# Layer 2: the queries' low parts on 128 rows through DMA copies, multiplies on GpSimd, another order of work; layer 3: the minimum that starts from the sink

## The chip, the cores and the metric

The kernel runs on one core of one Trainium2 chip. The metric is the device time of one execution in microseconds. In the texts TensorE (PE in the profile; its weight loads are PEld) multiplies matrices, VectorE (DVE), ScalarE (ACT) and GpSimd (POOL) work on vectors, and SyncE (SP) issues most of the DMAs. Each of them works through its own queue in order.

## What is computed

The kernel computes two blocks behind each other, of two layers each, on 512 tokens of width 1024 (32-bit floats): layer 1 (a gated recurrence and pooling), layer 2 (attention over the best keys), then layer 3 (attention in a window, with sinks), a feed-forward layer, layer 4 (three kinds of attention) and a second feed-forward layer. The change touches layers 2 and 3. Of the reference, layer 2 in its core:

```python
q = rmsnorm(q.reshape(hd), g_q)                 # 16 heads of 64
ckv = rmsnorm(ckv, g_kv)                        # rank 256
k = rmsnorm((ckv @ w_uk).reshape(hd), g_k)
v = (ckv @ w_uv).reshape(hd)
...
score = jnp.where((key_pos[None, :] <= t[:, None])[None], score, -jnp.inf)
_, idx = lax.top_k(score, top_k)                # 128 keys for each query
...
logits = jnp.einsum('bqhd,bqkhd->bqhk', qb, ksel).astype(jnp.float32) * (C_HEAD_DIM ** -0.5)
logits = logits + bias.transpose(0, 1, 3, 2)
logits = jnp.where(valid[:, :, None, :], logits, -jnp.inf)
probs = jax.nn.softmax(logits, axis=-1).astype(v.dtype)
return jnp.einsum('bqhk,bqkhd->bqhd', probs, vsel)
...
return x + (out * jax.nn.silu(z)) @ w_out
```

and layer 3 in its core (a window of 128 keys; `sk` is the sink, one number for each head):

```python
m = jnp.maximum(jnp.max(s, axis=-1, keepdims=True), sk)
e = jnp.exp(s - m)
p = e / (jnp.sum(e, axis=-1, keepdims=True) + jnp.exp(sk - m))
return jnp.einsum('bhgqs,bshd->bqhgd', p.astype(vn.dtype), vn)
```

## The kernel before

Matmuls are made of two halves of each number. An operand is split into a high part (h) and a low part (l), and a dense product is three matmuls: high by high, low by high, high by low (lines 148 to 150). Weights come by DMA from SP into `raw` (line 124), ScalarE writes the high part `wh` (line 129) and another engine subtracts for the low part `wl` (line 130); in layers 2 and 3 that engine is GpSimd. There are two `raw` buffers and four pairs of `wh` and `wl`.

Layer 2 is `odd`. TensorE's order is the order in which the code is written; the other engines' order follows from a scheduler. A `Filler` holds a list of work items (projections of queries, keys, values and gates, and parts of the output product), and `f.fill(n)` lets TensorE do the next n parts of it. An item's weights are asked for when the item before it begins. `mid` hangs a function between two parts of an item, here the transposes `q_t` and `k_t`, which bring queries and keys to feature-major form (`to_feature`, line 960: TensorE transposes, line 965, then the split). Between the parts stands first the choice of the keys (`topk`: 16 rounds of a maximum and a replacement on VectorE, lines 895 and 896), which ends in a mask for each block of 128 queries, and then the attention.

Queries and keys leave the projection token-major. `head_scale` (line 933) squares them (ScalarE), adds up (VectorE), takes the power -0.5 on GpSimd (`rr`, line 293) and multiplies by it (line 955).

The attention goes by units: one unit is one head and one half of the queries (256 rows: two blocks of 128), 32 units in all, by four groups g of four heads. Half 0 has 128 and 256 keys for its two blocks, half 1 has 384 and 512. The first group takes its eight units half by half, the later ones pair by pair. In step s of the loop TensorE does the logits of unit s, then two parts of the filler, the values of unit s - 3, the transposes of the probabilities of unit s - 2, and two parts again. `attend` (line 714) has the logits, the reduction with the bias strip (line 736), the exponential (line 738), the reciprocal (line 740) and the scaling by it, of the first block on VectorE (line 742) and of the second on ScalarE (line 743).

A head has 64 rows. The keys tile of one head `kT[g][j][r]` holds its high part in 64 rows and its low part in the other 64. A logit tile is two matmuls (`qk2r`, line 776): the high part of the queries, doubled over 128 rows (`qd`), by the whole keys tile, and the low part, 64 rows, by the high part of the keys:

```python
pe.matmul(lg, qd[:, o:o + P], k[:, :S], start=True, stop=False)
pe.matmul(lg, ql[rows, bs], k[rows, :S], start=False, stop=stop)
```

`query_twice` (line 1128) makes `qd` by two GpSimd copies of 64 x 256 a unit (line 1135), one unit ahead, into two buffers. Where queries are masked, a bf16 matmul adds the mask (line 732).

Layer 3 is `swa`; its units (`unit`, line 1287) are one head and one half, 32 again. GpSimd puts the negated sink `nsk` into a column beside the logits (line 1295), VectorE reduces each block with the strip to its minimum (all is negated; line 1304), takes the minimum with the sink (line 1306), ScalarE makes the exponentials (line 1309), VectorE the reciprocal (line 1310) and the scaling of both blocks (line 1313); TensorE transposes them three units later (line 1318).

Of the kernel before, what the change touches and what calls it, by code (L numbers as in the profile page):

```python
# [11 lines left out]
F32R = mybir.dt.float32r  # L12
# [4 lines left out]
P = 128  # L17
# [9 lines left out]
def f32(ap):  # L27
    return ap.bitcast(F32)
# [3 lines left out]
def kernel(ctx: ExitStack, tc: tile.TileContext, a: dict, out: bass.AP, upto: int = 9, start: int = 1):  # L32
# [681 lines left out]
    def attend(half, lp, qk, strip, probs, mask=None, gate=None, lbufs=2):  # L714
# [24 lines left out]
            Ls.append(L)  # L739
        dve.reciprocal(sm[:, 4:6], sm[:, 2:4])  # L740
        if gate is None:
            dve.tensor_scalar(Ls[0], Ls[0], sm[:, 4:5], None, op0=ALU.mult)
            act.activation(Ls[1], Ls[1], AF.Copy, scale=sm[:, 5:6])
        else:
            for ii in range(2):
                (dve if ii == half else pool).tensor_scalar(Ls[ii], Ls[ii], sm[:, 4 + ii:5 + ii], gate(i0 + ii),
                                                            op0=ALU.mult, op1=ALU.mult)
# [25 lines left out]
                pe.matmul(dst[:, :, 256 - w:], vv(b), p[:, :, 256 * b:256 * b + w], start=start and x + b == 0,  # L773
                          stop=stop and x == 1 and b == nb - 1)

    def qk2r(qd, ql, k, r, half):


        rows = slice(64 * r, 64 * r + 64)

        def f(lg, i, S, stop):
            bs, o = slice(i * P, (i + 1) * P), (i - 2 * half) * P
            pe.matmul(lg, qd[:, o:o + P], k[:, :S], start=True, stop=False)
            pe.matmul(lg, ql[rows, bs], k[rows, :S], start=False, stop=stop)
        return f

    def qk2(q, k):
# [21 lines left out]


    def odd(n):
        es, lp, tmp = open_layer("l2", 0, 0, 5, dict(mm=2, at=2, lg=2, po=2), weng=[pool])
        use_mm("lg", "po")

        def rt(name):
# [117 lines left out]
        def head_scale(ps, name, pre):  # L933
# [18 lines left out]
                dve.tensor_mul(r4, r4, pre[:, 0:NB, None].to_broadcast([P, NB, 4]))  # L952
            for x in range(2):
                t8 = tt[x].rearrange("p (h d) -> p h d", d=64)
                dve.tensor_mul(t8, t8, r[:, 8 * x:8 * x + 8, None].to_broadcast([P, 8, 64]))
            return [t[:, o:o + 256] for t in tt for o in (0, 256)]

        kT, qT, vv = {}, {}, {}
# [106 lines left out]
        with tc.manual_schedule(engines={pe.engine}):  # L1065
# [10 lines left out]
            def k_t(g, j):  # L1076
                return to_feature("kt", kT, g, gqk, j)

            f = Filler([proj(3, index_query), proj(0, latent), proj(1, latent), queries(0), keys(0), zgate(0),
                        mid(zgate(1), {2: q_t(0, 0), 5: q_t(0, 1)}), mid(zgate(2), {1: k_t(0, 0), 5: k_t(0, 1)}),  # L1080
                        values(0), zgate(3), zgate(4), zgate(5),
                        keys(1), mid(queries(1), {11: k_t(1, 0), 15: k_t(1, 1)}), values(1), keys(2),
                        mid(queries(2), {0: q_t(1, 0), 12: q_t(1, 1), 13: k_t(2, 0), 15: k_t(2, 1)}), values(2),
                        mid(out_part(0, 0), {4: q_t(2, 0)}), mid(out_part(0, 1), {2: q_t(2, 1)}), keys(3),
                        mid(queries(3), {10: k_t(3, 0), 11: k_t(3, 1)}), values(3),
                        mid(out_part(1, 0), {2: q_t(3, 0), 4: q_t(3, 1)}), zgate(6), out_part(1, 1), zgate(7),
                        out_part(2, 0), out_part(2, 1)])
            n.rtm
            f.fill(7)
# [38 lines left out]
            def query_twice(s):  # L1128
                if s in qd or s >= len(units) or len(qT.get(units[s][0], ())) <= units[s][1]:
                    return  # L1130
                g, j, half, r = units[s]
                rows = slice(64 * r, 64 * r + 64)
                t = qd[s] = lp.tile([P, 256], F32R, tag="qd", name="qd", bufs=2)
                for x in range(2):
                    pool.tensor_copy(t[64 * x:64 * x + 64], qT[g][j][0][rows, 256 * half:256 * half + 256])

            for s in range(len(units) + 3):
                query_twice(s)
                if s < len(units):
                    g, j, half, r = units[s]  # L1140
                    w = 256 * (half + 1)
                    stp = lp.tile([P, w], F32, tag=f"stp{half}", name="stp", bufs=2)
                    nc.sync.dma_start(stp, strip_ap(0, 4 * g + 2 * j + r, 1, T - w, w))

                    def probs(s=s, half=half):
                        pr[s] = prob_tiles(lp, half, 1, 1)
                        return [p[:, 0] for p in pr[s]]

                    live.append(attend(half, lp, qk2r(qd.pop(s), qT[g][j][1], kT[g][j][r], r, half), stp, probs,
                                       masks, lbufs=2))  # L1150
                    next(live[s])
                f.fill(2 if s < 24 else 1.4)
                query_twice(s + 1)
                if s >= 3:
                    u = s - 3
                    g, j, half, r = units[u]
# [64 lines left out]
    def swa(n):  # L1221
# [65 lines left out]
        def unit(j, r, half):  # L1287
# [13 lines left out]
                pe.matmul(d, q[r][:, bs], k[0][:, ks], start=True, stop=False)  # L1301
                pe.matmul(d, q[r][:, bs], k[1][:, ks], start=False, stop=True)
            for ii, (c0, S) in enumerate(where):
                dve.tensor_tensor_reduce(LL[:, c0 + ii:c0 + ii + S], lg[:, c0:c0 + S], strip[:, h, 256 - S:], 1.0, -NEG,
                                         op0=ALU.add, op1=ALU.min, accum_out=sm[:, ii:ii + 1])
            dve.tensor_scalar(sm[:, 0:2], sm[:, 0:2], nsk[:, h:h + 1], None, op0=ALU.min)
            for ii, (c0, S) in enumerate(where):
                L = LL[:, c0 + ii:c0 + ii + S + 1]
                act.activation(L, L, AF.Exp, scale=-1.0, bias=sm[:, ii:ii + 1], accum_out=sm[:, 2 + ii:3 + ii])
            dve.reciprocal(sm[:, 6:8], sm[:, 2:4])  # L1310
            for ii, (c0, S) in enumerate(where):
                L = LL[:, c0 + ii:c0 + ii + S]
                dve.tensor_scalar(L, L, sm[:, 6 + ii:7 + ii], None, op0=ALU.mult)
            yield
            pt = ps_at("pt")
            for x in range(3 + half):
# [711 lines left out]
```

## Time and profile before

| | us |
|---|---|
| three runs | 1972.92, 1973.52, 1975.42 (median 1973.52) |
| the profiled execution | 1972.96 |
| its span, first to last instruction | 1970.9 |
| busy: TensorE | 1917.8 (97%) |
| busy: VectorE | 1292.7 (66%) |
| busy: ScalarE | 964.6 (49%) |
| busy: GpSimd | 532.8 (27%) |

A busy share is a mean over stages with different limits, so it has to be asked for stage by stage. Layer 2 lies between about 490 and 780 us of the span, its attention between 570 and 760; layer 3's attention lies between 820 and 920. [...] Matmuls lie over each other, so what one costs is read from its start to the start of the next. A wait is put down to the instruction that came last.

### The profile page before, as it was taken

The numbers are of one execution on the slowest core, as the hardware profiler recorded it, in microseconds if no ns is written. First come the engines' busy times: TensorE is split into PE (matmuls) and PEld (weight loads), VectorE is DVE, ScalarE is ACT, GpSimd is POOL, SyncE is SP. The second block draws the span as 40 slices with busy tenths as digits, with TensorE's granted clock in tenths as the row PEclk, the third lists the DMA queues.
The fourth block names the chain that finished last, engine by engine and source line by source line (L and its number), as shares of the span: only waits on it lengthen the run. The fifth ranks groups of instructions, "written<-read, shape, count | busy, mean of one in ns | idle before, by whom it ended". The sixth has DMA issues, their size and how long they took to land.

```text
span 1970.9 us, 27008 instructions
## 1 busy us (share of the span) xinstructions
PE 1917.8 (97%) x9669; PEld 1595.5 (81%) x9678; DVE 1292.7 (66%) x2679; ACT 964.6 (49%) x1976; POOL 532.8 (27%) x612
## 2 busy tenths in 40 slices
PE   9999999999899999899999999998999999999998
PEld 7888888887787877777888888887888888888887
DVE  6776667556997777597654454456999765445443
ACT  5543343434447776586432232345888653323233
POOL 1101011025554545654200000044666440000002
PEclk9999999999999999899999999999999999999999
DMA  4233332213233332211423223233211132322321
GB/s 160 90 109 106 126 112 97 97 65 102 83 106 94 98 94 99 92 53 33 140 96 96 93 93 98 76 126 104 71 44 39 43 134 93 96 95 96 97 80 59
DMA packets 62063, 181.37 MB, mean 92 GB/s; under 512 B 7077, under 2 KB 13477, under 8 KB 61929
## 3 DMA queue, kind: packets, MB, share of 16 engines
q1 hardware_dynamic: 58200, 175.90, 28.0%
q10 hardware_dynamic: 3728, 3.75, 0.6%
q8 instruction: 76, 1.25, 0.3%
q14 instruction: 59, 0.48, 0.1%
HBM read 167.03 MB, written 12.59 MB: 91 GB/s over the span
## 4 chain that ended last, share of the span: by engine, by line
PE 83%; DVE 12%; ACT 2%; issue 1%; POOL 1%; DMA 1%; DVEq 0%; ACTq 0%; POOLq 0%
PE pj L148 6%; PE pj L149 6%; PE pj L150 6%; PE pg L149 4%; PE pg L148 4%; PE pg L150 4%; PE pu L149 4%; PE pu L148 4%; PE pu L150 4%; PE dn L149 4%; PE dn L148 4%; PE dn L150 4%; PE wo L148 3%; PE wo L150 3%; PE wo L149 3%; PE po L773 2%
## 5 line engine op out<-in xcount | busy, mean ns | idle before, releaser
L129 ACT CAST wh<-raw 128x512 fp32r<-128x512 f32 (+1 forms) x582 | 354.2, 613 | 620.4 <-PE pu L149 140.5
L130 DVE TENSOR_TENSOR wl<-raw,wh 128x512 fp32r<-128x512 f32 (+2 forms) x425 | 291.2, 689 | 189.8 <-ACT wh L129 187.6
L148 PE MATMUL pj<-xh,wh 128*128 128x512 f32 (+1 forms) x648 | 267.2, 413 | 2.1 <-DVE gx L1570 1.6
L150 PE MATMUL pj<-xh,wl 128*128 128x512 f32 (+1 forms) x648 | 257.1, 397 | 2.9 <-POOL wl L130 2.9
L149 PE MATMUL pj<-xl,wh 128*128 128x512 f32 (+1 forms) x648 | 257.2, 397 | 1.5 <-DVE xl L277 1.5
L130 POOL TENSOR_TENSOR wl<-raw,wh 128x512 fp32r<-128x512 f32 x157 | 208.0, 1328 | 172.9 <-ACT wh L129 156.9
L150 PEld LDWEIGHTS pj<-xh,wl 128*128 128x128 f32 (+1 forms) x648 | 122.8, 190 | 31.9 <-POOL wl L130 3.7
L285 POOL TENSOR_TENSOR sq<-sq 128x512 f32<-128x512 f32 x30 | 47.5, 1582 | 366.7 <-ACT sq L283 366.3
L148 PEld LDWEIGHTS pj<-xh,wh 128*128 128x128 f32 (+1 forms) x648 | 123.6, 191 | 24.8 <-ACT wh L129 2.0
L149 PEld LDWEIGHTS pj<-xl,wh 128*128 128x128 f32 (+1 forms) x648 | 123.4, 190 | 24.8 <-DVE xl L277 2.9
L149 PE MATMUL dn<-hl,wh 128*128 128x512 f32 (+1 forms) x376 | 141.6, 377 | 0.0
L148 PE MATMUL dn<-hh,wh 128*128 128x512 f32 (+1 forms) x376 | 141.2, 377 | 0.0
L150 PE MATMUL dn<-hh,wl 128*128 128x512 f32 (+1 forms) x376 | 140.7, 375 | 0.0
L148 PE MATMUL pg<-xh,wh 128*128 128x512 f32 x352 | 138.2, 393 | 0.0
L149 PE MATMUL pg<-xl,wh 128*128 128x512 f32 x352 | 138.2, 393 | 0.0
L150 PE MATMUL pg<-xh,wl 128*128 128x512 f32 x352 | 138.2, 393 | 0.0
L148 PE MATMUL pu<-xh,wh 128*128 128x512 f32 x352 | 138.0, 392 | 0.0
L150 PE MATMUL pu<-xh,wl 128*128 128x512 f32 x352 | 138.0, 392 | 0.0
L149 PE MATMUL pu<-xl,wh 128*128 128x512 f32 x352 | 137.9, 392 | 0.0
L148 PE MATMUL wo<-yh,wh 128*128 128x512 f32 x320 | 130.4, 408 | 0.9 <-DVE x L318 0.9
L149 PE MATMUL wo<-yl,wh 128*128 128x512 f32 x320 | 125.6, 393 | 0.0
L150 PE MATMUL wo<-yh,wl 128*128 128x512 f32 x320 | 125.4, 394 | 0.0
(413 smaller groups left out, 4403.5 us busy)
## 6 DMA issues: line engine op xcount, KB each, us to landing
raw<-in_w_gu SPq DMA_DIRECT2D x88, 512.0 KB, 3.5
raw<-in_w_even SPq DMA_DIRECT2D x48, 512.0 KB, 3.6
raw<-in_w_dn SPq DMA_DIRECT2D x32, 512.0 KB, 3.5
rsc<-rv SPq DMA_DIRECT2D x64, 160.0 KB, 3.7
raw<-in_w_eout SPq DMA_DIRECT2D x16, 512.0 KB, 3.6
stp<-rsc SPq DMA_DIRECT2D x32, 256.0 KB, 2.7
raw<-in_w_odd SPq DMA_DIRECT2D x13, 512.0 KB, 3.7
raw<-in_w_dn SPq DMA_DIRECT2D x16, 384.0 KB, 3.0
```

The lines of the kernel that those rows point to most:

```text
L129: act.copy(h[:, :m], raw[:, o:o + m])
L130: eng[i % len(eng)].tensor_sub(l[:, :m], raw[:, o:o + m], f32(h[:, :m]))
L148: pe.matmul(ps, wh, xh, start=first, stop=False)
L149: pe.matmul(ps, wh, xl, start=False, stop=False)
L150: pe.matmul(ps, wl, xh, start=False, stop=last)
L285: (eng or (dve if k == KD - 1 else pool)).tensor_add(n.sq[0], n.sq[0], sq)
L773: pe.matmul(dst[:, :, 256 - w:], vv(b), p[:, :, 256 * b:256 * b + w], start=start and x + b == 0, stop=stop and x == 1 and b == nb - 1)
```

## The change

In layer 2:

- `qd` holds the high and the low part of the queries, each doubled over 128 rows, and both matmuls of a logit tile have 128 rows of weights. The low part now also meets the low part of the keys.
- `qd` is made by four DMAs a unit on SP, into three buffers, up to two units ahead, and no longer by GpSimd.
- The two head-scale multiplies and the scaling of a unit's first block go from VectorE to GpSimd.
- The filler's items stand in another order: queries before keys, and the transposes `q_t` and `k_t` in other places. There are seven buffers for temporaries in place of five.

In layer 3:

- The reduction begins with the sink's column instead of a constant, and the separate minimum goes.
- The scaling of a unit's first block goes from VectorE to GpSimd.

```diff
@@ attend
-            dve.tensor_scalar(Ls[0], Ls[0], sm[:, 4:5], None, op0=ALU.mult)
+            pool.tensor_scalar(Ls[0], Ls[0], sm[:, 4:5], None, op0=ALU.mult)
             act.activation(Ls[1], Ls[1], AF.Copy, scale=sm[:, 5:6])
@@ qk2r
-    def qk2r(qd, ql, k, r, half):
-        rows = slice(64 * r, 64 * r + 64)
+    def qk2r(qd, k, half):
         def f(lg, i, S, stop):
-            bs, o = slice(i * P, (i + 1) * P), (i - 2 * half) * P
-            pe.matmul(lg, qd[:, o:o + P], k[:, :S], start=True, stop=False)
-            pe.matmul(lg, ql[rows, bs], k[rows, :S], start=False, stop=stop)
+            o = (i - 2 * half) * P
+            pe.matmul(lg, qd[:, 0, o:o + P], k[:, :S], start=True, stop=False)
+            pe.matmul(lg, qd[:, 1, o:o + P], k[:, :S], start=False, stop=stop)
         return f
@@ odd
-        es, lp, tmp = open_layer("l2", 0, 0, 5, dict(mm=2, at=2, lg=2, po=2), weng=[pool])
+        es, lp, tmp = open_layer("l2", 0, 0, 7, dict(mm=2, at=2, lg=2, po=2), weng=[pool])
@@ head_scale
-                dve.tensor_mul(t8, t8, r[:, 8 * x:8 * x + 8, None].to_broadcast([P, 8, 64]))
+                pool.tensor_mul(t8, t8, r[:, 8 * x:8 * x + 8, None].to_broadcast([P, 8, 64]))
@@ the filler's items
-                        mid(zgate(1), {2: q_t(0, 0), 5: q_t(0, 1)}), mid(zgate(2), {1: k_t(0, 0), 5: k_t(0, 1)}),
-                        values(0), zgate(3), zgate(4), zgate(5),
-                        keys(1), mid(queries(1), {11: k_t(1, 0), 15: k_t(1, 1)}), values(1), keys(2),
-                        mid(queries(2), {0: q_t(1, 0), 12: q_t(1, 1), 13: k_t(2, 0), 15: k_t(2, 1)}), values(2),
-                        mid(out_part(0, 0), {4: q_t(2, 0)}), mid(out_part(0, 1), {2: q_t(2, 1)}), keys(3),
-                        mid(queries(3), {10: k_t(3, 0), 11: k_t(3, 1)}), values(3),
-                        mid(out_part(1, 0), {2: q_t(3, 0), 4: q_t(3, 1)}), zgate(6), out_part(1, 1), zgate(7),
+                        zgate(1), mid(zgate(2), {1: q_t(0, 0), 5: q_t(0, 1)}),
+                        values(0), mid(zgate(3), {1: k_t(0, 0), 5: k_t(0, 1)}), zgate(4), zgate(5),
+                        queries(1), keys(1), values(1), mid(keys(2), {0: q_t(1, 0), 3: k_t(1, 0)}),
+                        mid(queries(2), {8: q_t(1, 1), 10: k_t(1, 1), 13: k_t(2, 0), 15: k_t(2, 1)}), values(2),
+                        mid(out_part(0, 0), {6: q_t(2, 0)}), mid(out_part(0, 1), {6: q_t(2, 1)}), queries(3), keys(3),
+                        mid(values(3), {2: q_t(3, 0)}), mid(out_part(1, 0), {3: k_t(3, 0), 7: k_t(3, 1)}),
+                        mid(zgate(6), {1: q_t(3, 1)}), out_part(1, 1), zgate(7),
@@ query_twice
-                t = qd[s] = lp.tile([P, 256], F32R, tag="qd", name="qd", bufs=2)
-                for x in range(2):
-                    pool.tensor_copy(t[64 * x:64 * x + 64], qT[g][j][0][rows, 256 * half:256 * half + 256])
+                t = qd[s] = lp.tile([P, 2, 256], F32R, tag="qd", name="qd", bufs=3)
+                for y in range(2):
+                    for x in range(2):
+                        nc.sync.dma_start(f32(t[64 * x:64 * x + 64, y]), f32(qT[g][j][y][rows, 256 * half:256 * half + 256]))
+            query_twice(0)
             for s in range(len(units) + 3):
                 query_twice(s)
+                query_twice(s + 1)
...
                 f.fill(2 if s < 24 else 1.4)
-                query_twice(s + 1)
+                query_twice(s + 2)
@@ unit, layer 3
-                dve.tensor_tensor_reduce(LL[:, c0 + ii:c0 + ii + S], lg[:, c0:c0 + S], strip[:, h, 256 - S:], 1.0, -NEG,
-                                         op0=ALU.add, op1=ALU.min, accum_out=sm[:, ii:ii + 1])
-            dve.tensor_scalar(sm[:, 0:2], sm[:, 0:2], nsk[:, h:h + 1], None, op0=ALU.min)
+                dve.tensor_tensor_reduce(LL[:, c0 + ii:c0 + ii + S], lg[:, c0:c0 + S], strip[:, h, 256 - S:], 1.0,
+                                         nsk[:, h:h + 1], op0=ALU.add, op1=ALU.min, accum_out=sm[:, ii:ii + 1])
...
-                dve.tensor_scalar(L, L, sm[:, 6 + ii:7 + ii], None, op0=ALU.mult)
+                (pool if ii == 0 else dve).tensor_scalar(L, L, sm[:, 6 + ii:7 + ii], None, op0=ALU.mult)
```

GpSimd's queue in layer 2, from the power for the first group's queries on (`rr`); `wl` are the low parts of weights. Before:

```order
L293 TENSOR_TENSOR rr<-rv,mhalf 128x16
L130 TENSOR_TENSOR wl<-raw,wh 128x512 x2
L293 TENSOR_TENSOR rr<-rv,mhalf 128x16
L1135 COPY qd<-qth 64x256 x4
L130 TENSOR_TENSOR wl<-raw,wh 128x512 x10
L1135 COPY qd<-qth 64x256 x2
L130 TENSOR_TENSOR wl<-raw,wh 128x512
```

and after:

```order
L293 TENSOR_TENSOR rr<-rv,mhalf 128x16
L130 TENSOR_TENSOR wl<-raw,wh 128x512
L293 TENSOR_TENSOR rr<-rv,mhalf 128x16
L130 TENSOR_TENSOR wl<-raw,wh 128x512
L953 TENSOR_TENSOR qt<-qt,rr 128x512 x2
L953 TENSOR_TENSOR kt<-kt,rr 128x512 x2
L130 TENSOR_TENSOR wl<-raw,wh 128x512 x11
L742 TENSOR_SCALAR L<-L,sm 128x128 x2
```

The copies are gone; the multiplies of queries and keys stand behind both powers and two weight splits, and the scalings follow.

SP's queue where the first group's attention begins; `stp` are bias strips, `rsc` a table written for layers 3 and 4, the `raw` loads are weights. Before:

```order
L124 DMA raw<-in_w_uv 128x512
L693 DMA rsc_4596<-rv 16x4x640
L1143 DMA stp<-rsc_915 128x256 x2
L124 DMA raw<-in_w_uk 128x512
L693 DMA rsc_4596<-rv 16x4x640
L124 DMA raw<-in_w_oq 128x1024
```

and after:

```order
L1134 DMA qd<-qth 64x256 x2
L1134 DMA qd<-qtl 64x256 x2
L1144 DMA stp<-rsc_915 128x256
L124 DMA raw<-in_w_uv 128x512
L1134 DMA qd<-qth 64x256 x2
L1134 DMA qd<-qtl 64x256 x2
L1144 DMA stp<-rsc_915 128x256
L1134 DMA qd<-qth 64x256 x2
L1134 DMA qd<-qtl 64x256 x2
L693 DMA rsc_4596<-rv 16x4x640
L124 DMA raw<-in_w_uk 128x512
```

Between two weight loads there now stand four to eight copies, each with waits of its own.

VectorE's queue in layer 3's attention, about one unit (the two-column minimum is line 1306). Before:

```order
L1306 TENSOR_SCALAR sm<-sm,nsk 128x2
L110 TENSOR_TENSOR p3l<-pt,p3h 128x384
L1310 RECIPROCAL sm<-sm 128x2
L1313 TENSOR_SCALAR L<-L,sm 128x256 x2
L1304 ISA L,sm<-lg,strip 128x128
```

and after:

```order
L1305 ISA L,sm<-lg,strip,nsk 128x128
L1305 ISA sm 128x1
L1305 ISA L,sm<-lg,strip,nsk 128x256
L1305 ISA sm 128x1
L1310 RECIPROCAL sm<-sm 128x2
L110 TENSOR_TENSOR p3l<-pt,p3h 128x384
L1313 TENSOR_SCALAR L<-L,sm 128x256
```

The minimum is gone, the reduction reads the sink's column, and one scaling of two is left.

## Rows read from the trace of the kernel before

**Rows 1.** Stages, length; busy (count): PE, PEld, DVE, ACT, POOL; PEclk, DMA share, GB/s.

```profile
500.00:594.00 94.00, 85.23 (x495) 73.15 (x493) 92.15 (x225) 43.78 (x88) 51.51 (x46) 0.96 0.34 102
536.00:540.00 4.00, 2.43 (x8) 1.93 (x9) 4.00 (x10) 1.25 (x3) 2.60 (x3) 0.55 0.53 176
613.00:763.00 150.00, 146.69 (x911) 120.15 (x918) 115.81 (x292) 112.11 (x254) 73.51 (x84) 1.00 0.31 92
826.00:880.00 54.00, 48.73 (x289) 40.51 (x289) 53.25 (x185) 47.50 (x129) 32.12 (x41) 1.00 0.14 50
880.00:920.00 40.00, 36.30 (x204) 29.31 (x203) 37.84 (x125) 29.84 (x79) 18.57 (x22) 1.00 0.10 30
```

**Rows 2.** Timeline of PE, layer 2 units: start, duration, line, out<-in, rows*columns of weights, output.

```profile
639.88 0.42 PE L783 MATMUL lg<-ktl,qd 128*128 128x384 f32 x1
640.23 0.44 PE L784 MATMUL lg<-ktl,qtl 64*128 64x384 f32 x1
640.60 0.34 PE L732 MATMUL lg<-mask,identb 128*128 128x384 bf16 x1
640.64 0.53 PE L783 MATMUL lg<-ktl,qd 128*128 128x512 f32 x1
641.10 0.50 PE L784 MATMUL lg<-ktl,qtl 64*128 64x512 f32 x1
641.56 0.47 PE L993 MATMUL pv<-wh,ckvh 128*128 128x256 f32 x1
...
645.38 0.23 PE L783 MATMUL lg<-kth,qd 128*128 128x128 f32 x1
...
646.42 0.28 PE L732 MATMUL lg<-mask,identb 128*128 128x256 bf16 x1
```

**Rows 3.** Timeline of PE, one logit tile pair of layer 4.

```profile
1436.71 0.33 PE L791 MATMUL lg<-kdh,ql 128*128 128x384 f32 x1
...
1437.05 0.39 PE L791 MATMUL lg<-kdh,ql 128*128 128x512 f32 x1
...
1437.52 0.49 PE L756 MATMUL pt<-cst,L 128*128 128x128 f32 x3
```

**Rows 4.** DVE by line and shape: count, busy us, mean ns, idle before.

```profile
L742 DVE TENSOR_SCALAR L<-L,sm 128x384 f32<-128x384 f32 x16 | 7.3, 453 | 0.4
L742 DVE TENSOR_SCALAR L<-L,sm 128x128 f32<-128x128 f32 x16 | 6.9, 431 | 0.4
L955 DVE TENSOR_TENSOR kt<-kt,rr 128x512 f32<-128x512 f32 x8 | 6.4, 843 | 0.0
L955 DVE TENSOR_TENSOR qt<-qt,rr 128x512 f32<-128x512 f32 x8 | 5.2, 686 | 0.0
L1306 DVE TENSOR_SCALAR sm<-sm,nsk 128x2 f32<-128x2 f32 x32 | 14.6, 457 | 0.3
L1313 DVE TENSOR_SCALAR L<-L,sm 128x256 f32<-128x256 f32 x48 | 23.3, 513 | 0.2
```

**Rows 5.** Waits of PE, 440 to 960 us: us in total, times, longest.

```profile
PE tf L965 <- DVE qt L955: 3.4, 1, 3.4
PE tf L965 <- DVE kt L955: 2.3, 2, 1.2
```

**Rows 6.** POOL by line and shape, columns as in rows 4, with releasers.

```profile
L130 POOL TENSOR_TENSOR wl<-raw,wh 128x512 fp32r<-128x512 f32 x157 | 208.0, 1328 | 172.9 <-ACT wh L129 156.9 <-DVE sm L740 5.5 <-issue 3.3
L1135 POOL CAST qd<-qth 64x256 fp32r<-64x256 f32 x64 | 28.8, 450 | 42.6 <-PE lg L783 32.8 <-ACT qth L109 5.6 <-ACT wh L129 2.2
L746 POOL TENSOR_SCALAR L<-L,sm,G 128x384 f32<-128x384 f32 x32 | 24.3, 759 | 18.5 <-DVE sm L740 18.1
L293 POOL TENSOR_TENSOR rr<-rv,mhalf 128x16 f32<-128x16 f32 x8 | 23.2, 2906 | 5.2 <-DVE sm L740 3.1 <-DVE rv L291 2.0
L746 POOL TENSOR_SCALAR L<-L,sm,G 128x256 f32<-128x256 f32 x32 | 18.5, 579 | 11.2 <-DVE sm L740 11.1
```

**Rows 7.** DMA issues: out<-in, queue, count, KB each, median us to landing.

```profile
stp<-rsc SPq DMA_DIRECT2D x32, 256.0 KB, 2.7
```

More of the change, by code (lines that the diff above doesn't have):

```diff
@@ L1147, in probs @@
                         return [p[:, 0] for p in pr[s]]
-                    live.append(attend(half, lp, qk2r(qd.pop(s), qT[g][j][1], kT[g][j][r], r, half), stp, probs,
+                    live.append(attend(half, lp, qk2r(qd.pop(s), kT[g][j][r], half), stp, probs,
                                        masks, lbufs=2))
```

## The prediction, made before the changed kernel ran

> **What bounds the kernel now.** I read first the busy times by stage. In layer 2's last part, 613 to 763 us, TensorE is busy 146.69 of 150 us and the next, VectorE, 115.81: TensorE sets the pace. [...] Then I read TensorE's own timeline in one attention unit, start to start, because the durations of pipelined matmuls overlap. Last come the prices of what moves, by shape.
>
> In layer 2 the two matmuls of a logit tile alternate between 128 rows of weights (line 783) and 64 rows (line 784). A unit of the second half takes 641.56 - 639.88 = 1.68 us with its mask matmul in it, a unit of the first half 646.42 - 645.38 = 1.04 us [rows 2]. Layer 4 has the same four shapes (384, 384, 512, 512 columns), all with 128 rows: 1437.52 - 1436.71 = 0.81 us [rows 3]. Each change between 64 and 128 rows costs about 0.2 us.
>
> **The change part by part.** The profiled execution took 1972.96 us (span 1970.9); the median of the runs is 1973.52, 0.03% above. The sum is made against 1972.96.
>
> *128 rows.* A second-half unit becomes 0.81 us plus its mask. The mask's price is between 0.04 (640.60 to 640.64) and 0.17 us (a 384-column matmul in layer 4) [rows 2, 3], so 0.85 to 0.98, a gain of 0.70 to 0.83. A first-half unit has two matmuls of 128 and two of 256 columns. In [rows 3] 384 columns take 0.17 and 512 take 0.235, so 256 take 0.11 to 0.12 and 128 take 0.04 to 0.06: 0.30 to 0.36 in all. The mask behind it, now hidden, may cost 0.07 more, so the gain is 0.61 to 0.74. Over 16 units of each kind that is 21 to 25 us. I take 0.65 a unit, 21 us, near the lower end, since the mask rows are the less certain. The eight units of the first head group (5 us of the 21) lie before 613 us, where VectorE leads; the other 24 are worth 15.6 us on the path.
>
> [...] What the rows show is that a 64-row matmul does not lie over its neighbour: 0.37 us (384 columns) and 0.46 us (512) go by before the next one starts [rows 2]. [...]
>
> *VectorE's stretch, 500 to 613 us.* It is full, so what leaves VectorE shortens it. The head-scale multiplies (line 955) leave: in this stretch four of kt at 0.843 and four of qt at 0.686 us, 6.1 us. The probability scaling (line 742) of eight units leaves: 4 x 0.431 + 4 x 0.453 = 3.5 us [rows 4]. Together 9.6 us. TensorE must then also be early enough: it loses 5 us of row changes and has 8.8 us of idle time in 500 to 594 alone [rows 1]. One wait stays, I think: the transposes of the first qt waited 3.4 us [rows 5]. They move seven projection steps later, 7 x 3 matmuls of 0.235 us = 4.9 us, but the multiply they wait for goes to the end of GpSimd's chain: power 2.9, split 1.3, power 2.9, split 1.3 and two multiplies of 1.3 us [rows 6] (the order is shown with the change), where before VectorE did it right behind the first power. That is some 4 us later, so nothing is gained there. GpSimd's two-tensor price is that of its split, 1.328 us for 128x512 [rows 6], twice VectorE's. I take 9 us for the stretch. Bounds: 4, if GpSimd's multiplies come late, to 11, if the waits for kt (2.3 us [rows 5]) and a stretch of half clock go as well.
>
> *Layer 2, 613 to 763 us.* TensorE stays the bound: VectorE loses 24 scalings and 8 head-scale multiplies, 10.6 + 6.1 us, and falls to 99. ScalarE keeps 112.11 us [rows 1], 84% of some 134. GpSimd gives up 48 query copies of 0.450 (21.6 us, and with them most of the 32.8 us that it stood waiting for logit matmuls), and takes 12 scalings of 384 columns at 0.759, 12 of 128 at some 0.4 and 8 multiplies at 1.328, 24.5 us [rows 6]. So it stays near 76 of 134. I take 15 of the 15.6 us: spaced-out kt transposes give one or two back, and a pipeline that runs 10% faster over engines 84% full will wait now and then. Bounds 9 to 19.
>
> The query copies become 128 DMAs on SP, four a unit. Their cover is the lead: a unit's copy is issued two units ahead and needs only the logits of three units back, so it has two to three units of 150/24 = 6.2 us. It needs four issues and a landing, which I take from the strip's DMA, 2.7 us [rows 7]; with the issues at most 4 us. Cost taken: nothing; without the cover up to 4 us a unit. The weights queued behind them on SP are fetched a whole work item ahead.
>
> *Layer 3.* In 826 to 920 us TensorE idles 5.3 + 3.7 = 9 us while VectorE is full [rows 1]. The 32 two-column minima go (0.457 each, 14.6 us), and of the 64 scalings half: 24 x 0.513 + 8 x 0.28 = 14.6 us [rows 4]; the 0.28 for 128 columns is an estimate, half of the 0.513 for 256 and a little. VectorE falls from 91 to some 62 us. The reduction that now starts from a column instead of a constant keeps its price, at a guess within 0.05 us. Next in line are ScalarE, 47.5 of 54 us in the first part, and GpSimd, 32.12 plus some 18 scalings of 0.4 to 0.579 us, 9 us [rows 1, 6]. So in the first part I take 3.5 of 5.3 us, in the second 3.5 of 3.7: 7 us, bounds 3 to 10.
>
> **Sum:** 9 + 15 + 7 = 31 us, 1972.96 - 31 = **1942 us**.
>
> **Rivals.**
>
> 1. *GpSimd or ScalarE takes VectorE's place.* GpSimd works in order; a scaling that waits for a reciprocal holds up the splits behind it, and the transposes then wait for the scaling. Against it: GpSimd's load is 57% to 85%. It gives the lower bounds, 4 + 9 + 3 = 16 us: 1957 us. Chance 0.17.
> 2. *More than taken:* all upper bounds, 11 + 19 + 10 = 40 us: 1933 us. Chance 0.13.
> 3. *The change of rows is not what costs* (the change does not do what it says): the 0.2 us stay with the operands. For it: line 783, with 128 rows, is slow too. Against it: layer 4 with 128 rows on both has nothing of it [rows 3]. Then 15 us of the middle and 3 of the first stretch fall away: 13 us are left, 1960 us. Chance 0.07.
> 4. *The 64-row matmuls are hidden today.* As a mechanism here: the second matmul of each pair, 0.06 + 0.12 us in a first-half and 0.17 + 0.235 in a second-half unit [rows 3], would come into sight, 16 x 0.59 = 9.4 us, and the 21 us would not come. 1972.96 - 31 + 21 + 9.4 = 1972.4 us, no change. The start-to-start rows speak against it [rows 2]. Chance 0.03. [...]
> 5. *Slower: SP's queue.* SP issues in order; the four copies of a unit wait for older logit matmuls, for the query split and for a free buffer, and the next weights stand behind them. If the lead shrinks from 12 or more us to under 4, each unit waits for a landing. At 1 us a unit (32 us) the gain is gone; at 1.5 us it is 48 - 31 = 17 us slower, 1990 us. For it: the first units of a group have their queries only one to two units ahead. Against it: the lead above. Chance 0.05.
>
> **How the numbers follow.** The forecast, 1934 to 1952 (39 to 21 us, between the sums of the bounds), has 0.55; the rivals 0.17, 0.13, 0.07, 0.03 and 0.05. A range of 1931 to 1960 us takes in rivals 1 and 2 and half of 3, and leaves out 4, 5 and the tails, less than 0.2. A measurement of this kernel can tell about 0.2%, 4 us, from no change. Faster by more: 0.55 + 0.17 + 0.13 + 0.07 = 0.92; within: 0.03; slower: 0.05.
>
> **What would show it.** After the change both logit lines carry 128 rows, and a second-half unit takes 0.85 to 1.0 us from its first logit matmul to the one behind it, a first-half unit 0.3 to 0.4. Layer 2's last projection and the first of layer 3 come 24 us earlier; VectorE in 500 to 600 us stays near full, but the last top-k mask comes some 9 us earlier. In layer 3 TensorE's idle time shrinks from 9 to 2 us and VectorE falls to 70% or so. I am wrong if TensorE waits for a qd DMA or for weights that came late, if GpSimd becomes the longest wait of the transposes, if half-clock stretches appear that were not there, or if the 0.2 us gaps outlive the 64-row form.

## The result: 1953.47 us, and the profile after

The changed kernel takes 1953.47 us (median of four runs, 1950.72 to 1956.98) against 1973.22 us (four runs, 1972.06 to 1975.42). The ratio is 0.9898 with an interval of 0.9882 to 0.9913, a gain of 17 to 23 us. The forecast was 1942 us, a gain of 31; its wide range, 1931 to 1960, holds the result, while the forecast proper, 1934 to 1952, misses it by 1.5 us. The profiled execution of the changed kernel is the longest of its four runs, 1956.98 us (span 1955.3 us).

Layer 2 is read between three places that both kernels pass: the sums `cst` at 512 us, where they are still in step, the first logits of the second head group, and the first projection of layer 3. Columns as in [rows 1]. Before:

```profile
512.35:619.13 106.78, 98.62 (x599) 85.09 (x601) 100.44 (x242) 57.45 (x120) 57.82 (x53) 0.95 0.34 103
619.13:781.01 161.88, 158.57 (x945) 129.27 (x951) 125.18 (x300) 118.27 (x262) 82.19 (x88) 1.00 0.29 86
```

and after, with the two windows of layer 3 from [rows 1]:

```profile
512.23:616.88 104.65, 94.81 (x597) 83.26 (x597) 88.03 (x225) 55.02 (x117) 67.39 (x50) 0.95 0.48 133
616.88:773.15 156.27, 148.70 (x956) 129.62 (x955) 110.20 (x271) 118.81 (x265) 91.17 (x74) 0.98 0.43 124
826.00:880.00 54.00, 53.51 (x321) 45.12 (x320) 52.22 (x163) 50.04 (x135) 48.15 (x62) 1.00 0.16 50
880.00:920.00 40.00, 39.98 (x203) 32.99 (x202) 29.49 (x75) 26.07 (x61) 27.08 (x28) 1.00 0.12 41
```

In layer 3 TensorE has lost its idle time: 0.5 us of 94 are left, where [rows 1] has 9. In layer 2 it has more of it: up to the second head group 104.65 - 94.81 = 9.8 us (8.2 before), behind that 156.27 - 148.70 = 7.6 us (3.3 before), and there the granted clock is 0.98 where it was 1.00.

How far the layers came forward is read from three starts: the first logits of the second head group, the first projection of layer 3 (`kv`) and the last norm sums of layer 3 (`nst`). Timeline of PE of the kernel before, with one second-half unit (from its first logits to the matmul behind it):

```profile
619.13 0.22 PE L783 MATMUL lg<-kth,qd 128*128 128x128 f32 x1
...
656.80 0.34 PE L783 MATMUL lg<-kth,qd 128*128 128x384 f32 x1
...
658.40 0.58 PE L148 MATMUL wo<-yh,wh 128*128 128x512 f32 x1
...
781.01 0.40 PE L148 MATMUL kv<-xh,wh 128*128 128x512 f32 x1
957.10 0.95 PE L306 MATMUL nst<-cst,sq 128*128 128x2 f32 x8
```

The same three of the changed kernel, with one first-half unit and the same second-half unit between them:

```profile
616.88 0.22 PE L781 MATMUL lg<-kth,qd 128*128 128x128 f32 x1
...
648.27 0.22 PE L781 MATMUL lg<-ktl,qd 128*128 128x128 f32 x1
...
648.73 0.28 PE L732 MATMUL lg<-mask,identb 128*128 128x256 bf16 x1
...
654.43 0.34 PE L781 MATMUL lg<-kth,qd 128*128 128x384 f32 x1
...
654.82 0.53 PE L781 MATMUL lg<-kth,qd 128*128 128x512 f32 x1
655.19 0.40 PE L782 MATMUL lg<-kth,qd 128*128 128x512 f32 x1
...
655.47 0.58 PE L148 MATMUL wo<-yh,wh 128*128 128x512 f32 x1
...
773.15 0.40 PE L148 MATMUL kv<-xh,wh 128*128 128x512 f32 x1
939.33 0.95 PE L306 MATMUL nst<-cst,sq 128*128 128x2 f32 x8
```

The second head group starts 2.25 us earlier, layer 3 7.86 us earlier, its end 17.77 us earlier. So the stretch up to the second group gave 2.2 us, the rest of layer 2 5.6 us, layer 3 9.9 us. Behind layer 3, where the two kernels are the same, the profiled execution of the changed one takes 1955.3 - 939.33 = 1016.0 us against 1970.9 - 957.10 = 1013.8 us. So the two profiled executions lie 16.0 us apart, and the medians 19.8 us.

A second-half unit takes 655.47 - 654.43 = 1.04 us, where the same unit took 658.40 - 656.80 = 1.60 us before. The unit of [rows 2], 1.68 us, stands right behind transposes and is one of the longer ones: twelve of the sixteen took 1.59 to 1.61 us. A first-half unit takes 648.73 - 648.27 = 0.46 us (1.04 in [rows 2], between the same two rows).

TensorE's waits from 440 to 960 us (us in total, times, longest), those of layer 2:

```profile
PE tf L963 <- POOL kt L953: 2.9, 2, 2.6
PE tf L963 <- DVE pl L760: 2.8, 3, 1.9
...
PE tf L963 <- POOL qt L953: 2.5, 3, 1.8
PE pt L756 <- DVE ktl L971: 2.4, 1, 2.4
PE tf L963 <- DVE ktl L971: 2.3, 1, 2.3
...
PE pk L991 <- ACT qt L937: 2.0, 1, 2.0
...
PE pk L991 <- DVE vv L1013: 0.7, 1, 0.7
```

and two of the kernel before:

```profile
PE tf L965 <- DVE ktl L973: 2.1, 1, 2.1
...
PE pt L756 <- DVE ktl L973: 1.2, 2, 0.7
```

The 3.4 us on `qt` of [rows 5] shrank to 2.3 (2.5 with a later one). New are the waits on GpSimd's `kt`, on `pl`, and those of `pk` on `qt` and `vv`, where one projection hands its banks to the next. The waits on `ktl` were there before and have grown by 1.4 us. (The transposes `tf` of queries and keys share two banks with those of the probabilities, `pt`.)

### The profile page after: what moved, and what is told of

It is laid out like the page before. It is cut to its first block, busy times and chain, and to the rows that moved or that the text cites. A ratio compares the mean times of both kernels' runs of the same rounds, so it can differ in the third digit from the quotient of the medians.

```text
span 1955.3 us, 27178 instructions
## 1 busy us (share of the span) xinstructions
PE 1904.5 (97%) x9678; PEld 1596.7 (82%) x9678; DVE 1253.2 (64%) x2567; ACT 959.3 (49%) x1976; POOL 574.6 (29%) x628
## 4 chain that ended last, share of the span: by engine, by line
PE 87%; DVE 7%; ACT 3%; POOL 1%; issue 1%; DMA 1%; DVEq 0%; ACTq 0%; POOLq 0%
PE pj L148 7%; PE pj L149 7%; PE pj L150 7%; PE pg L149 4%; PE pg L148 4%; PE pg L150 4%; PE pu L148 4%; PE pu L149 4%; PE pu L150 4%; PE dn L149 4%; PE dn L148 4%; PE dn L150 4%; PE wo L148 4%; PE wo L150 4%; PE wo L149 4%; PE po L773 2%
```

## The experiments

Each ratio is to the kernel before, run on the same chip in the same rounds.

### The 128 rows alone

```diff
 kernel before, with only
+    qd = lp.tile([P, 2, 256], ..., bufs=3), filled by four DMAs a unit
+    pe.matmul(lg, qd[:, 0, o:o + P], k[:, :S], ...); pe.matmul(lg, qd[:, 1, o:o + P], k[:, :S], ...)
```

> Before, with the 128 rows and their DMA copies alone (filler, multiplies and layer 3 as before). If each change between 64 and 128 rows costs 0.2 us and TensorE is the bound from 613 us on: 24 units x 0.65 = 15.6 us on the path, and up to 5 more where VectorE leads: 1953 to 1960 us, and a second-half unit of 0.85 to 1.0 us in the trace. If the 0.2 us belong to the operands, or the gain is lost to other waits: 1968 to 1975. If the DMA copies come late: over 1975, and TensorE waits for qd.

Measured: 1966.32 us, 0.9963 (0.9951 to 0.9976): 5 to 10 us, between the two bands expected. The units are short, as expected (1.04 us), but in the order of before the copies are late, and TensorE waits for them. Waits of PE, 613 to 763 us:

```profile
PE lg L782 <- DMA qd<-qtl: 1.9, 2, 1.2
PE lg L781 <- DMA qd<-qth: 1.7, 1, 1.7
```

Of the 3.6 us on `qd`, 2.9 stand at the start of the second group: this order transposes that group's queries at 614.82 us, a unit ahead of their use at 621.76. The changed kernel transposes them at 601 us, 16 us ahead of their use, and has no wait on `qd`.

### Layer 3 alone, and the sink alone

```diff
 kernel before, with only
-            dve.tensor_scalar(sm[:, 0:2], sm[:, 0:2], nsk[:, h:h + 1], None, op0=ALU.min)
+            (the reduction begins with nsk[:, h:h + 1])
-                dve.tensor_scalar(L, L, sm[:, 6 + ii:7 + ii], None, op0=ALU.mult)
+                (pool if ii == 0 else dve).tensor_scalar(L, L, sm[:, 6 + ii:7 + ii], None, op0=ALU.mult)
```

> Before, with layer 3's part of the change alone. The prediction: 7 us, 1966. The trace of the changed kernel lets me expect 10 us, since TensorE's waits there are almost gone: 1963. If GpSimd takes VectorE's place: 1970 or more.

The second kernel has the sink only; both scalings stay on VectorE.

> The kernel before with the third layer's minimum beginning with the sink alone; both multiplications of the probabilities stay on VectorE. It takes 32 small operations of 0.46 us, 14.6 us, from VectorE, and one step from each unit's chain. Theory A (the step in the chain is what counts): most of the 12.8 us of the whole third part, so 1962 to 1965 us. Theory B (VectorE's load counts, and GpSimd's multiplications take the larger share of it): 1967 to 1971 us.

Measured: both parts 1960.66 us, 0.9935 (0.9923 to 0.9948), 10 to 15 us, more than the 7 of the prediction and the 10 expected here; the sink alone 1964.6 us, 0.9951 (0.9938 to 0.9963), 7 to 12 us, in the band of theory A. Stage 783 to 930 us, columns as in [rows 1], of before, of both parts, and of the sink alone:

```profile
783.00:930.00 147.00, 132.59 (x697) 108.71 (x696) 117.99 (x356) 99.39 (x248) 86.49 (x96) 0.97 0.21 69
```

```profile
783.00:930.00 147.00, 140.69 (x737) 116.80 (x736) 112.58 (x298) 104.66 (x258) 119.53 (x134) 0.97 0.22 73
```

```profile
783.00:930.00 147.00, 138.05 (x724) 114.19 (x723) 115.70 (x327) 102.63 (x254) 91.89 (x100) 0.97 0.22 70
```

The sink alone takes 5.5 of the 8.1 us that TensorE's idle time loses. The minima and the scalings take about the same 14.6 us from VectorE by the sum of the prediction, so its load alone does not explain why the sink brings more; the step taken out of each unit's chain can. That is not shown: the scalings were not tried alone, and what the sink leaves for them to win is less. Layer 3's part was sized too low.

### The changed kernel with the low part on 64 rows

```diff
-            pe.matmul(lg, qd[:, 1, o:o + P], k[:, :S], start=False, stop=stop)
+            pe.matmul(lg, ql[rows, bs], k[rows, :S], start=False, stop=stop)
```

> After, with the low part on 64 rows again, straight from the query tile (two DMA copies a unit in place of four). If the rows are worth what the timeline shows, 1953.5 + 12 to 16 = 1965 to 1970 us. If in the new order other waits decide (transposes of queries and keys), the rows are hidden behind them: 1953 to 1959.

Measured: 1963.13 us, 0.9941 (0.9928 to 0.9955), between the two bands. In the changed kernel's order the rows are worth 0.9941 - 0.9898 = 0.0043, 8.5 us (4 more or less, by the two intervals). And without them this kernel, with the new order, GpSimd's multiplies and layer 3's part, can't be told from layer 3's part alone (0.9935).

### Two changes of rows in a unit instead of four

```diff
-            for each block: 128-row matmul, 64-row matmul, mask
+            both 128-row matmuls, both 64-row matmuls, both masks   (second halves only)
```

> Before, with the four logit matmuls of a second-half unit in another order: both of 128 rows, then both of 64 rows, then the masks. Same matmuls, same rows, two changes of row count a unit in place of four. If the change of rows costs: 0.4 us a unit, 16 units, of them 12 behind 613 us: 4.8 us, 1968, and 1.68 us become some 1.3. If the 64-row form itself or its operands cost: 1973 and 1.68 us as before.

Measured: 1972.16 us, 0.9995 (0.9986 to 1.0003), near the 1973 of the second theory, while the unit is as the first has it. Timeline of PE, one such unit:

```profile
659.11 0.57 PE L798 MATMUL lg<-kth,qd 128*128 128x384 f32 x2
659.61 0.67 PE L800 MATMUL lg<-kth,qtl 64*128 64x384 f32 x2
...
660.41 0.58 PE L148 MATMUL wo<-yh,wh 128*128 128x512 f32 x1
```

The unit takes 1.30 us instead of 1.60: with two changes fewer it is 0.30 us shorter, so a change of row count costs, and 0.15 us is its price. Over 16 units TensorE has 4.8 us less to do, and at most 2.8 of them show in the time. Layer 3 begins at 781.03 us, as before. In this trace some 3.4 of the 4.8 us are lost again: from the sums `cst` to layer 3 TensorE is idle 13.2 us where it was 11.5, and from 642 to 646 us the clock is at 0.65 and 0.50 (two windows of 2 us, 1.7 us lost), where before it was 1.00. One more thing blurs this: in the grouped order the first block's logits are ready only behind all four matmuls (its mask matmul begins 1.10 us behind the unit's first logits, 0.65 before), so VectorE's work on it can start only later.

### The parts together without the new order; the new order taken back; the head-scale multiplies back on VectorE

```diff
 first:  kernel before + the 128 rows + layer 3's part
 second: changed kernel, the filler's items in the order of before
 third:  changed kernel, with
-                pool.tensor_mul(t8, t8, r[:, 8 * x:8 * x + 8, None].to_broadcast([P, 8, 64]))
+                dve.tensor_mul(t8, t8, r[:, 8 * x:8 * x + 8, None].to_broadcast([P, 8, 64]))
```

> The kernel before with two parts of the change only: 128 rows with the queries doubled by DMA, and the third layer's part. The order of the filler work and the multiplications in the second layer stay as before. Theory A (the parts add, and the new order and GpSimd's multiplications in the second layer are worth nothing): 7.2 us from the rows alone and 12.8 us from the third layer alone, so some 1954 us (1952 to 1956), the same as the whole change. Theory B (the new order makes room for the rows, and the rows bring more with it): over 1957 us.

> The changed kernel with the filler work of the second layer in the order of before; rows, copies, GpSimd's multiplications and the third layer as changed. Theory A (the order is worth nothing either way, since each order has its own waits of TensorE): 1951 to 1956 us. Theory B (the new order covers GpSimd's slower multiplications, 1.07 us where VectorE took about 0.8): 1957 us or more, with longer waits of the transposes for the queries and keys. Theory C (the new order costs, since it puts the projections of queries, keys and values behind each other and each waits for the banks of the one ahead, 2.0, 0.9 and 0.7 us at 585 to 602 us): 1948 to 1950 us.

> The changed kernel with the 16 multiplications of the head norms of queries and keys back on VectorE; the one of the probabilities stays on GpSimd. Theory A (layer 2 is paced by TensorE, and its transposes wait on GpSimd's multiplications, 5.4 us in the profiled run): these waits go and the time falls by 3 to 5 us, to 1949 to 1951 us. Theory B (VectorE still sets the pace ahead of 570 us and gives back some 4 of the multiplications' 12 us): 1956 to 1960 us. Nothing either way (each wait is replaced by the next): 1952 to 1955 us.

Measured: 1957.52 us, 0.9911 (0.9897 to 0.9924); 1956.43 us, 0.9903 (0.9888 to 0.9918); 1955.37 us, 0.9902 (0.9888 to 0.9915). The changed kernel's 0.9898 (0.9882 to 0.9913) can't be told from any of the three: it is faster by 2.6, 1.0 and 0.8 us, each 4 more or less. So it isn't shown that the new order and GpSimd's multiplies are worth anything. Of the theories named ahead, that the new order costs and that the multiplies back on VectorE gain 3 to 5 us are out; between the others the intervals don't decide. The old order has its own waits, 4.0 us on `qd`.

The third run shows what the head-scale multiplies do. The last top-k mask on VectorE's timeline, before (with the multiplies behind it), changed, and with the multiplies back:

```profile
589.84 0.42 DVE L901 TENSOR_SCALAR mask<-s 128x512 bf16<-128x512 f32 x1
...
590.18 2.35 DVE L955 TENSOR_TENSOR kt<-kt,rr 128x512 f32<-128x512 f32 x2
```

```profile
580.44 0.81 DVE L899 TENSOR_SCALAR mask<-s 128x384 bf16<-128x384 f32 x2
```

```profile
588.71 0.41 DVE L899 TENSOR_SCALAR mask<-s 128x512 bf16<-128x512 f32 x1
...
588.76 0.48 PE L732 MATMUL lg<-mask,identb 128*128 128x384 bf16 x1 [7.70 <-DVE mask L899]
```

The masks are done at 590.26, 581.25 and 589.12 us: the 9 us are there, and 7.9 of them go when the multiplies come back. With the multiplies back TensorE stands 7.7 us for the mask, and the end is still the same within the intervals: each of the two kernels waits, at another place.

### The projections spread out

The waits at 585, 592 and 604 us (`qt`, `kt`, GpSimd's `kt`) come from one place: the second group's queries and keys stand directly behind each other in the filler's list.

```diff
-                        values(0), mid(zgate(3), {1: k_t(0, 0), 5: k_t(0, 1)}), zgate(4), zgate(5),
-                        queries(1), keys(1), values(1), mid(keys(2), {0: q_t(1, 0), 3: k_t(1, 0)}),
+                        values(0), mid(zgate(3), {1: k_t(0, 0), 5: k_t(0, 1)}), queries(1), zgate(4), keys(1),
+                        zgate(5), values(1), mid(keys(2), {0: q_t(1, 0), 3: k_t(1, 0)}),
```

> The changed kernel with one thing altered in the second layer's filler list: the projections of the second group's queries and keys are put between the three gate projections ahead of them instead of directly behind each other, so that they stand some 10 to 20 us earlier and no two projections that need both banks meet. Theory A (TensorE paces layer 2, and each of its waits costs its own length and the half clock that follows it): the waits at 585, 592 and 604 us go, 2.0 + 0.9 + 2.6 us, with about 2.6 us of half clock at 604 to 612, so 5 to 8 us, 1946 to 1949 us. Theory B (what TensorE gains it waits for later, on the work of VectorE and ScalarE in the units): 1952 to 1956 us with new waits of the same sum.

Measured: 1947.99 us (1946.92 to 1949.80), 0.987 (0.9855 to 0.9885), some 5.5 us faster than the changed kernel (4 more or less, by the two intervals), in the band of theory A; layer 3 begins at 765.82 us, 7.3 us earlier. The two stretches of layer 2:

```profile
512.00:612.16 100.16, 93.13 (x597) 82.91 (x597) 88.96 (x224) 54.85 (x116) 65.60 (x48) 0.97 0.47 133
612.16:765.82 153.66, 145.91 (x957) 127.21 (x955) 110.41 (x270) 118.54 (x265) 92.98 (x77) 1.00 0.46 131
```

Up to the second group TensorE is idle 7.0 us instead of 9.8; behind it 7.75 us, as in the changed kernel (7.57). So less waiting gives some 2.6 of the 7.3 us, as expected. The rest is half-clock time: the clock is 0.97 instead of 0.95 in the first stretch, and 1.00 instead of 0.98 in the second, which was not expected. That the order brings this part, too, is not shown: the two profiled executions lie 10.1 us apart, the medians 5.5.

### Every transpose placed anew; only three of them moved

```diff
 first, on the spread order: all of
+  mid(values(1), {1: q_t(1, 0)}), mid(keys(2), {1: k_t(1, 0)}),
+  mid(queries(2), {8: q_t(1, 1), 12: k_t(1, 1), 15: k_t(2, 0)}), mid(values(2), {2: k_t(2, 1)}),
+  ... mid(out_part(0, 1), {4: q_t(2, 1)}), ... mid(values(3), {0: q_t(3, 0)}), mid(out_part(1, 0), {0: k_t(3, 0), 4: k_t(3, 1)})
 second, on the spread order: only
+  mid(values(2), {1: k_t(2, 1)}), mid(out_part(1, 0), {0: q_t(3, 0), 3: k_t(3, 0)}), mid(zgate(6), {1: q_t(3, 1), 5: k_t(3, 1)})
```

> As the run with the projections spread, and the transposes of queries and keys are moved, too, to units whose probabilities need only one transposed bank (first halves), so that they meet the two shared banks free. Theory A: of the waits on pl and ktl, 7.1 us in the profiled run of the changed kernel, 4 to 6 go as well, with some 3 us of half clock behind them: 1940 to 1946 us. Theory B (the sum of the waits stays): 1952 to 1956 us.

> As the run with the projections spread (1948.0 us), with three transposes moved one to three units later: the second half of the third group's keys behind its values (it waited 2.28 us on the first half's bank), the fourth group's queries into the output projection behind (1.95 us on pl), its keys' second half into the gate projection behind that (2.41 us of a unit's transposes on ktl). Theory A (waits of TensorE are what is left between this kernel and the full worth of the rows): 4 to 7 us, so 1941 to 1944 us. Theory B (each moved transpose meets another wait, as in the run with all of them placed anew, 1950.6 us): 1947 to 1951 us.

Measured: 1950.63 us, 0.9887 (0.987 to 0.9903), between the two bands, and 1947.43 us, 0.9874 (0.9861 to 0.9888), in the band of theory B. Neither beats the spread order. Waits of PE, 560 to 770 us, one row of each, first of the spread order, then with three transposes moved:

```profile
...
PE tf L963 <- DVE ktl L971: 2.5, 2, 2.3
...
```

```profile
PE tf L963 <- POOL kt L953: 3.6, 2, 3.0
...
```

The wait of `tf` on `ktl` is gone, and one on GpSimd's `kt` of 3.6 us has come. The sum over all rows is 12.3 us in the one and 12.5 in the other. Here the theory that every wait taken away is time won has fallen: three waits were moved, and others of the same sum took their place.

### The spread order with the low part on 64 rows

```diff
 as the spread order, with
-            pe.matmul(lg, qd[:, 1, o:o + P], k[:, :S], start=False, stop=stop)
+            pe.matmul(lg, ql[rows, bs], k[rows, :S], start=False, stop=stop)
```

> The run with the projections spread (1948.0 us), but with the logits' low part on 64 rows as before, from the queries themselves; the copies of the high part go by DMA. What the 128 rows are worth in an order with fewer waits. Theory A (each change of rows costs about 0.2 us whatever stands around it, and only waits hid part of it): nearer to the gaps' 16.7 us than the 10 us found in the changed kernel's own order, so 1961 to 1965 us. Theory B (about half of the gaps is always given back): 1956 to 1959 us.

Measured: 1961.91 us, 0.9946 (0.9933 to 0.996), in the band of theory A. The rows are worth 0.9946 - 0.987 = 0.0076, 15 us, in this order (again 4 more or less), 8.5 us in the changed kernel's (4 more or less), 7.3 us in that of before (5 to 10). Without the rows, the spread order is no better than the changed one (0.9946 against 0.9941).

The traces show where the two orders differ. The two stretches of layer 2 with the low part on 64 rows, first in the changed kernel's order, then in the spread order:

```profile
513.51:614.99 101.48, 97.26 (x594) 83.53 (x597) 87.64 (x225) 54.74 (x117) 67.63 (x50) 0.97 0.41 123
614.99:786.22 171.23, 164.84 (x951) 134.37 (x956) 111.52 (x271) 119.70 (x265) 90.67 (x74) 0.96 0.33 97
```

```profile
513.36:615.98 102.62, 97.18 (x597) 83.31 (x597) 89.17 (x224) 54.86 (x116) 65.92 (x49) 0.97 0.42 122
615.98:782.86 166.88, 160.47 (x954) 131.19 (x955) 110.97 (x270) 119.87 (x265) 92.64 (x76) 0.99 0.34 100
```

Behind the second group's start the 128 rows bring 171.23 - 156.27 = 15.0 us in the changed order and 166.88 - 153.66 = 13.2 us in the spread one. Ahead of it they bring 2.5 us in the spread order, and the changed one gets 3.2 us longer by them: TensorE's idle time rises there from 4.2 to 9.8 us, where the projections hand over their banks. These are single executions.

## Why the prediction was right in its sign, and where a third of its gain went

**The rows: right, and sized somewhat high.** The forecast priced a unit's gain at 0.61 to 0.83 us and took 0.65. A second-half unit gained 1.60 - 1.04 = 0.56, a first-half unit 0.58 us: 16 x 0.56 + 16 x 0.58 = 18.2 us of TensorE's own time, where 21 stood. (The signs named for the units, 0.85 to 1.0 and 0.3 to 0.4 us, are missed a little, at 1.04 and 0.46.) Two sizes were missed in the second halves: [rows 2] shows a unit that took 0.08 us more than most, and between the two 512-column matmuls there are now 0.37 us (654.82 to 655.19), longer than the 0.235 of [rows 3]. Four changes of row count went from each unit, so one costs 0.14 to 0.15 us, where the forecast said some 0.2; the grouped order gave 0.15. The rival that the 64-row matmuls are hidden today is out, and so is the one that the price belongs to the operands.

**VectorE's stretch, 9 us: the step that failed.** The mask came 9.0 us earlier, as the sum had it, and the second group started only 2.25 us earlier, although the 128 rows of the first group alone save 8 x 0.57 = 4.6 us of TensorE's time. The step took VectorE's full share for the bound and added what leaves it. But TensorE does all of layer 2's matmuls in one fixed order, and it can win only the time in which it stands. It never stood for the mask before: the last one was done at 590.26 us, and the first unit that needs it began at 592.78. It stood for `qt`, 3.4 us, for `kt`, 2.3 us, whose multiplies came right behind that mask (590.18) [rows 5], and for banks. That idle time had to be the term, with a name for each wait and its end, and it did not shrink: it went from 8.16 to 9.84 us. 4.6 - 1.7 = 2.9 us, near the 2.25 measured.

**The rest of layer 2, 15 us: mis-sized.** It was 5.6. The 24 units gained 24 x 0.57 = 13.7 us. TensorE's idle time rose by 7.57 - 3.31 = 4.3 us, and the clock cost 3.4 us: in windows of 2 us it is below 1.00 from 636 to 642 and from 712 to 718 us, 1.7 us lost in each. 13.7 - 4.3 - 3.4 = 6.0. The forecast had "one or two" us for waits, and nothing for the clock, since [rows 1] shows 1.00 there. Most of the new idle time comes with the other parts of the change (the order, the copies, the work moved to GpSimd), and not from TensorE being faster: with the low part on 64 rows the changed kernel has 171.23 - 164.84 = 6.4 us of it, with 128 rows 7.6. GpSimd's scaling of 384 columns took 1.28 us, too, where 0.759 was taken from another layer [rows 6].

**The copies' cover: right for this order.** TensorE has no wait on `qd`, and a copy lands 2.0 to 2.3 us behind its issue (medians, 560 to 770 us). The order of before, with the same copies, has 3.6 us, by the mechanism of the rival on SP's queue.

**Layer 3, 7 us: too low.** It gave 9.9 us (7.86 to 17.77), near the bound of 10, and 10 to 15 us where it was tried alone. The sum took 3.5 of 5.3 us of idle time in the first part, with ScalarE and GpSimd as the next limits; all but 0.5 us of both parts went. GpSimd and ScalarE run at 48.15 and 50.04 of 54 us without holding TensorE up. VectorE fell to 87% of the two parts and not to some 70%: they hold more work now, its scaling of 256 columns took 0.705 us where 0.513 stood, and its reduction of 256 columns 0.475 us where it had taken 0.417.

Two of the signs named ahead of the run as those of being wrong are in the trace: GpSimd as the longest wait of the transposes (2.9 us), and new half-clock stretches. They are the first rival's mechanism, GpSimd in VectorE's place, but with a smaller part than it was given: with the multiplies back on VectorE the time is the same within 4 us.

That the gain came to 20 of 31 us is in part luck. In the profiled execution layer 2 gave 7.9 of the 24 us forecast for it, and layer 3, sized 3 to 6 us too low, made up for a part. The first rival's 1957 us is nearer to the result than the forecast's 1942.

What stays open: whether the rows are worth more in the spread order (15 us) than in the changed kernel's (8.5); the two intervals overlap, and the stretch ahead of the second group is where the traces differ. Waits and clock account for the changed kernel, as above; how much of the clock is the order's doing, and how much the single execution's, these runs don't tell. The changed kernel's four runs stand in the order of their mean granted clock, from 0.987 at 1956.98 us to 0.992 at 1950.72; that their spread comes from the clock is likely, and not shown.

## What to carry to other kernels

Time taken off an engine that works through a fixed order is worth what its waits leave of it (in layer 2 here, 18.2 us off the matmuls and 7.9 off the time): list each wait of that engine with its releaser, and ask which of them moves when the engine comes earlier, before the gains are added. A second engine that is busy all the time is to be taken for a bound only where the first is seen to wait for its last result (here that result, the mask, came 9.0 us earlier, and what followed 2.25). Where work is put into gaps by a list, keep two steps that hand over the same buffers apart; that went with some 5 us here (4 more or less), while shifting single steps only moved the waits (12.3 us of them, then 12.5).

## What the runs showed of the hardware

*The same wait, with and without a slower clock.* The transposes of the keys stand 2.29 us on `ktl` in the changed kernel and 2.28 us in the spread order, with the same matmuls on both sides. Timeline of PE behind them, and the clock in windows of 2 us, changed kernel:

```profile
636.82 0.63 PE L963 MATMUL tf<-cst,kt 128*128 128x128 f32 x4 [2.29 <-DVE ktl L971]
...
637.70 0.88 PE L781 MATMUL lg<-ktl,qd 128*128 128x512 f32 x1
```

```profile
638.00:640.00 2.00, 2.00 (x8) 1.39 (x7) 1.37 (x4) 2.00 (x5) 1.41 (x2) 0.50 0.00 0
```

and the spread order:

```profile
632.09 0.63 PE L963 MATMUL tf<-cst,kt 128*128 128x128 f32 x4 [2.28 <-DVE ktl L971]
...
632.95 0.53 PE L781 MATMUL lg<-ktl,qd 128*128 128x512 f32 x1
```

```profile
632.00:634.00 2.00, 1.91 (x12) 1.48 (x13) 1.08 (x2) 2.00 (x6) 1.45 (x2) 1.00 0.01 4
```

In the one the clock is at 0.50 right behind the wait, and a 512-column matmul takes 0.88 us; in the other it stays at 1.00 and the matmul takes 0.53. The changed kernel's clock is below 1.00 from 636 to 642 us (0.92, 0.50 and 0.73 in three such windows), which is 0.16 + 1.00 + 0.54 = 1.7 us of lost time. With the low part on 64 rows the two kernels have the same wait again (2.27 us each): in the changed order the clock is 0.50 from 638 to 642 us behind it, and the 512-column matmul at 638.42 us takes 0.88 us; in the spread order the clock stays at 1.00, and that matmul, at 638.84 us, takes 0.53. So such a wait cost its length in the spread order, and in the changed order that and 1.7 us or more. Why the clock fell behind the one wait and not behind the other, no run here shows.

*Only beside a subtraction on GpSimd did VectorE's scalings run long; beside a scaling they stayed short.* VectorE's scaling of 128x256 took 0.513 us on average [rows 4] and takes 0.705 in the changed kernel, 0.697 in layer 3's part alone. Timeline of DVE, then of POOL, layer 3's part alone:

```profile
851.32 1.41 DVE L1312 TENSOR_SCALAR L<-L,sm 128x256 f32<-128x256 f32 x1
...
852.84 0.36 DVE L1312 TENSOR_SCALAR L<-L,sm 128x256 f32<-128x256 f32 x1
```

```profile
851.29 1.29 POOL L130 TENSOR_TENSOR wl<-raw,wh 128x512 fp32r<-128x512 f32 x1
852.56 0.78 POOL L1312 TENSOR_SCALAR L<-L,sm 128x128 f32<-128x128 f32 x1
```

The first scaling begins 0.03 us behind GpSimd's subtraction of two tensors and ends just behind it, after 1.41 us; the second runs beside a scaling of GpSimd and takes 0.36 us. In this trace eleven of VectorE's scalings ran beside a scaling of GpSimd and no subtraction, and took 0.35 to 0.39 us; those that met a subtraction took up to 1.46. In the changed kernel's trace it is ten with 0.34 to 0.39 us, and up to 1.50 for the 22 that met a subtraction. So what VectorE's scalings lose in these traces they lose beside subtractions on GpSimd, and not beside the scalings that went there; by what mechanism is not shown.
